# Keys and values of layer 1 in one 512-column product, the first output projection in two halves, a fourth weight slot

## The chip, the cores and the metric

The kernel runs on one core of one Trainium2 chip. A core has TensorE (PE, with its weight loads shown apart as PEld), VectorE (DVE), ScalarE (ACT), GpSimd (POOL), and SyncE (SP), whose queue issues most DMA transfers. Each engine takes its instructions in a fixed order. The metric is the device time of one execution in microseconds.

## The reference

Two transformer layers over 512 latent tokens and 256 context tokens, width 1024. Both normalize with adaptive scale and shift, project, attend, multiply by a SiLU gate, project out, normalize again and add to the stream. Layer 0 is differential attention with 8 heads, layer 1 grouped-query attention with 8 query heads and 2 key/value heads.

```
h  = rms_norm(x,  pre_g[i]) * (1.0 + scale)  + shift
hc = rms_norm(xc, pre_g[i]) * (1.0 + cscale) + cshift
# layer 0
q, k, v, z = split(h @ w_in)                 # heads with two maps each
o = softmax(q1 k1) v - lam * softmax(q2 k2) v
y = (rms_norm(o, subln_g) * (1 - lam_init) * silu(z)) @ w_out[0]
# layer 1
q, k, v, z = split(h @ w_in)                 # widths 1024, 256, 256, 1024
q, k = rms_norm(q, qk_g[0]), rms_norm(k, qk_g[1])
y = (softmax(rope(q) rope(k)) v * silu(z)) @ w_out[1]
# both
x  = x  + gate  * rms_norm(y,  post_g[i])
xc = xc + cgate * rms_norm(yc, post_g[i])    # layer 0 only
```

The output is the latent stream (512 x 1024) after layer 1.

## The kernel before

Every float32 product is made of three fast ones: an operand is split into a rounded part (`hi`) and the remainder (`lo`), and `mm3` issues hi·hi, hi·lo and lo·hi. `tmm` (L155) issues a single matmul, so most of PE's work has that line.

Weights come through `WStream`. A key stands for one block of 128 x 1024 values; `wsplit` loads it with SP into a raw tile (two buffers, tag `raw`), ACT casts it to `whi` (L225), and DVE subtracts to get `wlo` (L219). POOL does that for keys 9 and 11, in four pieces. A block needs a slot, a pair `whi`/`wlo`, from its load to `release`. Three slots exist throughout (`WBUFS`). A further one exists during the first projections (in the pool `st`), another from layer 0's output projection to the end of keys and values (pool `bp`, for those keys alone), and one more from there to the end of the kernel (pool `t1q`). Blocks are taken strictly in the order in which they were added.

Eight PSUM banks are used: four by themselves (`bk`; `pj` takes the one that was given back longest ago, `close` gives it back, `trp` takes one for a short time), and two pairs (`sc`, `sc2`) for scores and transposes.

Layer 0 runs as one flow over heads. `flow` walks lists of steps (scores S, transposes of probabilities T, products with values M, normalizing X, modulation vectors A) with costs, lags and due times from the constants at the top, and fills the time between due steps with pieces of projections (`fill0`: queries and keys `qk`, values `v`, gates `z`). The steps A compute adaptive vectors in twelve groups (`grp_mm`, L835); `gate0_finish` makes the gate of layer 0 from two of them per half: it loads `ada_b` and `post_g` into raw tiles, copies the row to all partitions with two matmuls per side (L1131, L1132), adds (L1133) and multiplies (L1134) on DVE for side 0 (latent) and 1 (context).

The code's order is not the engines' order: when the program is built, a scheduler places each engine's instructions by priority, and `tc.high_priority(offset=...)` moves a group ahead by that many. `HOT`, `HOT0`, `HOT1`, `WARM` and `PRI` are such offsets.

The output projection of layer 0 goes in column groups `OUTC`: 256, 256 and 512 columns, each for six token tiles of 128 rows. The first group is computed for the first seven of eight row blocks while the last head is still at work (`out_early`, into `o_pre`: two `sc` pairs for the latent tiles, two `bk` banks for the context tiles), and finished after it. Each group is multiplied by the gate on DVE and its squares are summed on ACT; `part_sum` on POOL adds the sums of the first two groups. After the third group a tile is normalized and added to the stream (`resid_a`, `resid_b`), and `h1_tr` transposes two tiles at a time (L1350) into the input of layer 1. The two context tiles (pair 2 of `h1_tr`, `t` in `KV`) are transposed among the key and value products.

The list `KV` orders that stage: `k` and `v` are 256-column products of one token tile (`proj_tok`, 8 row blocks x 3 matmuls), `t` transposes of context tiles, `c` transposes of finished keys (`k_tr`). Blocks 8 and 9 hold the key columns (4 row blocks of 256 columns each), 10 and 11 the value columns.

```
wk = (ws.get(8), ws.get(9))
...
o = pj(256)
run(proj_tok(o, wk if what == "k" else wv, m))
```

Then follow the queries of the first pair of heads and the attention flow of layer 1, built like that of layer 0, and its output projection (`OUTC1`).

Of the kernel before, what the change touches and what calls it, by code (L numbers as in the profile page):

```python
# [16 lines left out]
P = 128  # L17
# [11 lines left out]
HOT = -93  # L29
# [3 lines left out]
ACCN = (0, 0, 4, 2, 3, 2, 3, 4)  # L33
ACD = 0.54
FILL1 = (('q', 1), ('z', 0), ('z', 2), ('q', 2), ('z', 1), ('q', 3), ('z', 4), ('z', 5), ('z', 3), ('z', 6), ('z', 7))
HOT0 = (4682, 2421, 950, 3759)
HOT1 = (1476, 3151, 2600, 3663, 2938, 0)
WARM = 1817
AGB = 10
PRE = 16.26  # L40
# [3 lines left out]
KV = (('k', 0), ('k', 1), ('v', 0), ('k', 2), ('t', 0), ('k', 3), ('c', 0), ('v', 1), ('v', 2), ('t', 1), ('k', 4), ('c', 1), ('c', 2), ('k', 5), ('v', 3), ('v', 4), ('c', 3), ('c', 4), ('v', 5), ('c', 5))  # L44
SPL = 3.06
# [11 lines left out]
SLAG1 = 4.72  # L57
# [10 lines left out]
PRI = (1500, 218, 582, 400)  # L68
GFIN = (10, 13)
QLAG = 2.87  # L70
QTR = 5.35
# [6 lines left out]
RL = 3.57  # L78
# [9 lines left out]
def tile_backbone(  # L88
# [49 lines left out]
    def pj(n):  # L138
        i = lru.pop(0)
        o = banks[i][:, :n]  # L140
        held[id(o)] = (o, i)
        return o
# [136 lines left out]
    OUTC = ((0, 256), (256, 256), (512, 512))  # L279
# [9 lines left out]
    def wout_keys(layer, c, n):  # L289
        return [("o", layer, c, k) for k in range(KT * n // 1024)]  # L290

    def get_wout(layer, c, n):
        return [ws.get(k) for k in wout_keys(layer, c, n)]
# [518 lines left out]
    st_pool.close()  # L812

    gT = [None] * KT

    with tc.tile_pool(name="t0", bufs=1) as t0:
# [304 lines left out]
        def gate0_finish(half):  # L1121
            r = rows.pop((0, 4 + half))
            sl = slice(half * 512, half * 512 + 512)
            b = bcast(ada_b[0, 2 * D + half * 512:2 * D + half * 512 + 512])
            g = bcast(post_g[0, sl])
            rh, rl = (t0.tile([P, 512], F32R, tag="tmp", name=nm("rg"), bufs=3) for _ in range(2))
            nc.scalar.copy(rh, r)
            nc.vector.tensor_tensor(rl, r, f32(rh), ALU.subtract)
            for v in range(2):
                o = trp()  # L1130
                nc.tensor.matmul(o, selb[v], rh, start=True, stop=False)  # L1131
                nc.tensor.matmul(o, selb[v], rl, start=False, stop=True)  # L1132
                nc.vector.tensor_tensor(gate0[v][:, sl], o, b, ALU.add)  # L1133
                nc.vector.tensor_tensor(gate0[v][:, sl], gate0[v][:, sl], g, ALU.mult)  # L1134
# [135 lines left out]
    def proj_tok(o, w, t):  # L1270
        sl = slice(t * P, (t + 1) * P)
        for kt in range(KT):
            wh, wl = w[kt // 4]
            c = slice((kt % 4) * 256, (kt % 4) * 256 + 256)
            mm3(o, h1hi[:, kt, sl], h1lo[:, kt, sl], wh[:, c], wl[:, c], kt == 0, kt == KT - 1)
            yield 3 * 256 / 2400.0
# [8 lines left out]
    ws.extend(bp, WX[0], [*wout_keys(0, *OUTC[1]), *wout_keys(0, *OUTC[2]), 8, 9, 10, 11])  # L1285
# [7 lines left out]

    for qi, (c, n) in enumerate(OUTC[:2]):
        w = get_wout(0, c, n) if qi else w_o
        if qi == 0:
            for m in order:
                run(out_proj(o_pre[m], ghi, glo, w, m, n, KT - 1, KT))
        for m in order:
            v = 0 if m < NQ else 1  # L1300
            o = pj(n) if qi else o_pre[m]
            if qi:
                run(out_proj(o, ghi, glo, w, m, n))
            if qi == 0:
                u0[m] = hp.tile([P, 512], F32, tag="gT", name=nm("u0"), bufs=8)
                ss[m] = small(3)
            nc.vector.tensor_tensor(u0[m][:, c:c + n], o, gate0[v][:, c:c + n], ALU.mult)
            sumsq(ss[m][:, qi:qi + 1], o, n)
            if qi or m >= NQ:
                close(o)  # L1310
            if qi:
                part_sum(ss[m])
        ws.release(*wout_keys(0, c, n))
    c, n = OUTC[2]
# [63 lines left out]
    with tc.tile_pool(name="t1", bufs=1, side="right") as t1p:  # L1378
# [35 lines left out]
        wk = (ws.get(8), ws.get(9))  # L1414
# [24 lines left out]
        wv = None  # L1439
        for what, m in KV:  # L1440
            if what == "t":
                hot(h1_tr, 2, m)
            elif what == "c":
                k_tr(*ktr.pop(0))
            else:
                if what == "v" and wv is None:
                    wv = (ws.get(10), ws.get(11))
                o = pj(256)
                run(proj_tok(o, wk if what == "k" else wv, m))
                if late:  # L1450
                    k_rope(*late.pop())
                if what == "k":
                    late.append((m, o, head_rstd(o)))
                else:
                    nc.scalar.copy(vh[:, m, :], o)
                    nc.vector.tensor_tensor(vl[:, m, :], o, f32(vh[:, m, :]), ALU.subtract)
                    close(o)
# [3 lines left out]
        ws.extend(t1q, WX[1])  # L1461
# [354 lines left out]
```

## Time and profile before

| what | value |
| --- | --- |
| time, median of 3 runs (range) | 792.71 us (792.47 to 792.79) |
| time of the profiled execution | 792.77 us |
| its span, first to last instruction | 790.8 us |
| mean granted TensorE clock | 0.999 |
| DMA, mean over the span | 98 GB/s, 77.77 MB |
| PE's share of the chain that ended last | 89% |

The profile is of one execution. A page gives busy time of each engine, the costliest groups of instructions and the chain that ended last; further answers come from the same trace: busy time by stage, lists of waits, instructions in order of time. In a row of that last view stand start and length in us, engine, line, operation, tiles written and read, shape and count; in brackets the idle time before it and what ended it. Buffer numbers are left out in tile names. Ends of matmuls are modelled, starts are measured.

### The profile page before, as it was taken

The page shows a single profiled execution, that of the slowest core. Times are in us where ns is not written, and L with a number is a line of the kernel's source. Part 1 is how long each engine was busy: PE and PEld are TensorE (multiplying, and loading weights), DVE is VectorE, ACT ScalarE, POOL GpSimd, SP SyncE. Part 2 cuts the span into 40 slices and gives each one's busy share as a digit, 9 for nine tenths or more (in the row PEclk, how much of TensorE's full clock was granted, in tenths as well). Part 3 has the DMA queues.
Part 4 walks back from the last instruction along what each step waited for, and adds up shares of the span by engine and source line. Part 5 has one row for each costly group of instructions (what it writes and reads, how often), then busy time and mean ns, then how long its engine had stood idle before and what let it go on. Part 6 is the DMA issues. An engine that isn't in the chain of part 4 may idle for free.

```text
span 790.8 us, 14236 instructions
## 1 busy us (share of the span) xinstructions
PE 776.8 (98%) x5446; PEld 699.2 (88%) x5446; DVE 522.4 (66%) x940; ACT 455.4 (58%) x994; POOL 324.9 (41%) x434
## 2 busy tenths in 40 slices
PE   8999999999999999999999999999999999999996
PEld 6688888988887898888979998899999999989986
DVE  4666677786769637866578753567558977565634
ACT  5546546675575644775468843565456676676632
POOL 1121375663338542353425411585446654234101
PEclk9999999999999999999999999999999999999999
DMA  9934211131422322323330151041423512010102
GB/s 339 384 97 148 80 54 59 50 104 67 138 80 83 118 81 68 120 80 107 117 97 31 51 213 54 1 140 53 159 82 101 153 43 81 27 54 28 54 27 107
DMA packets 35092, 77.77 MB, mean 98 GB/s; under 512 B 3408, under 2 KB 10064, under 8 KB 35024
## 3 DMA queue, kind: packets, MB, share of 16 engines
q1 hardware_dynamic: 31168, 71.05, 26.9%
q10 hardware_dynamic: 3856, 5.81, 2.1%
q8 instruction: 43, 0.70, 0.3%
q14 instruction: 25, 0.20, 0.1%
HBM read 70.56 MB, written 2.10 MB: 92 GB/s over the span
## 4 chain that ended last, share of the span: by engine, by line
PE 89%; DVE 3%; ACT 3%; DMA 2%; POOL 1%; issue 1%; SPq 0%; DVEq 0%; ACTq 0%; POOLq 0%
PE bk L155 56%; PE sc L155 10%; PE bk L167 9%; PE sc L994 5%; PE bk L1059 3%; PE bk L1558 3%; PE bk L835 1%; DMA xnt<-in_xlT 1%; PE sc L1023 1%; POOL wlo L219 1%; DMA raw<-in_b_w 1%; DVE al L1063 1%; PE bk L406 1%; PE bk L407 1%; ACT p L1033 0%
## 5 line engine op out<-in xcount | busy, mean ns | idle before, releaser
L155 PE MATMUL bk<-whi,h 128*128 128x256 f32 (+1 forms) x1184 | 243.7, 299 | 0.0
L155 PE MATMUL bk<-h,whi 128*128 128x512 f32 (+2 forms) x864 | 227.9, 347 | 0.0
L155 PEld LDWEIGHTS bk<-whi,h 128*128 128x128 f32 x1184 | 191.8, 191 | 10.5 <-issue 4.0
L155 PE MATMUL bk<-wlo,h 128*128 128x256 f32 (+1 forms) x592 | 175.7, 299 | 0.0
L155 PEld LDWEIGHTS bk<-h,whi 128*128 128x128 f32 x864 | 149.9, 189 | 17.1 <-issue 2.9
L155 PE MATMUL bk<-h,wlo 128*128 128x512 f32 (+2 forms) x432 | 149.6, 346 | 0.0
L233 POOL TENSOR_SCALAR p<-p,sm 128x768 f32<-128x768 f32 (+1 forms) x80 | 71.7, 899 | 163.1 <-DVE sm L1005 63.9
L155 PEld LDWEIGHTS bk<-wlo,h 128*128 128x128 f32 x592 | 112.6, 191 | 3.8 <-issue 0.7
L219 DVE TENSOR_TENSOR wlo<-raw,whi 128x1024 fp32r<-128x1024 f32 (+1 forms) x66 | 80.7, 1226 | 34.4 <-ACT whi L225 34.3
L155 PEld LDWEIGHTS bk<-h,wlo 128*128 128x128 f32 x432 | 81.5, 189 | 7.1 <-issue 0.2
L225 ACT CAST whi<-raw 128x1024 fp32r<-128x1024 f32 x64 | 67.2, 1050 | 32.9 <-PE bk L155 27.8
L1002 ACT ACTIVATE p<-sc,sm 128x768 f32<-128x768 f32 (+1 forms) x68 | 59.5, 878 | 30.6 <-DVE sm L999 30.1
L999 DVE TENSOR_REDUCE sm<-sc 128x1 f32<-128x768 f32 (+1 forms) x68 | 60.3, 917 | 19.2 <-PE sc L994 19.2
L219 POOL TENSOR_TENSOR sz<-sz,za 128x192 f32<-128x192 f32 (+1 forms) x48 | 35.1, 752 | 65.8 <-ACT za L199 65.7
L1010 DVE SCALAR_TENSOR_TENSOR p<-p,sm,p 128x768 f32<-128x768 f32 (+1 forms) x34 | 40.3, 1186 | 7.4 <-POOL p L233 5.1
L994 PE MATMUL sc<-qk,qk 64*128 64x384 f32 (+1 forms) x396 | 43.8, 351 | 0.7 <-ACT p L1002 0.7
L1562 DVE TENSOR_TENSOR al<-bk,ah 128x512 fp32r<-128x512 f32 x48 | 32.1, 686 | 18.4 <-ACT ah L1561 18.2
L1062 ACT CAST ah<-bk 128x512 fp32r<-128x512 f32 x56 | 31.6, 589 | 19.0 <-PE bk L1059 16.6
L1063 DVE TENSOR_TENSOR al<-bk,ah 128x512 fp32r<-128x512 f32 x56 | 37.4, 683 | 6.7 <-ACT ah L1062 6.5
L1543 ACT ACTIVATE p<-sc,sm,qrs 128x768 f32<-128x768 f32 x32 | 31.9, 996 | 15.1 <-DVE sm L1540 8.9
L994 PEld LDWEIGHTS sc<-qk,qk 64*128 64x128 f32 x396 | 32.8, 184 | 7.7 <-issue 3.4
L1561 ACT CAST ah<-bk 128x512 fp32r<-128x512 f32 x48 | 26.9, 588 | 17.9 <-PE bk L1558 14.6
(240 smaller groups left out, 1492.6 us busy)
## 6 DMA issues: line engine op xcount, KB each, us to landing
raw<-in_a_w SPq DMA_DIRECT2D x28, 512.0 KB, 3.5
araw<-in_ada_w SPq DMA_DIRECT2D x12, 1024.0 KB, 5.2
raw<-in_b_w SPq DMA_DIRECT2D x20, 512.0 KB, 3.5
ag<-in_ada SPq DMA_DIRECT2D x16, 512.0 KB, 7.9
raw<-in_w_out SPq DMA_DIRECT2D x16, 512.0 KB, 3.5
sw<-qr ACTq DMA_DIRECT2D x32, 128.0 KB, 2.1
gw<-in_ada_w SPq DMA_DIRECT2D x8, 512.0 KB, 4.1
xnt<-in_xlT SPq DMA_DIRECT2D x4, 512.0 KB, 5.6
```

The source lines that it names most:

```text
L155: i = nc.tensor.matmul(o, a, b, start=start, stop=stop)
L167: nc.tensor.matmul(o, v[:, kt + e, c], a[:, e * 256:e * 256 + 256], start=first and i == 0, stop=last and i == 5)
L219: eng.tensor_tensor(dst[:, i:i + n], a[:, i:i + n], b[:, i:i + n], op)
L225: nc.scalar.copy(hi, r)
L233: (nc.vector if eng == "v" else nc.gpsimd).tensor_scalar(dst, src, s_, 1.0, ALU.mult, ALU.mult)
L994: prev = nc.tensor.matmul(sc[m][:, j if nk == T else m, :w], a[r, tok], b[r, c], start=i == 0, stop=i == 2)
L999: nc.vector.tensor_reduce(mx, scv, AX.XY if nk == T else AX.X, ALU.max, negate=True)
L1002: nc.scalar.activation(pv_, scv, AF.Exp, bias=mx, accum_out=l[:, m:m + 1])
L1010: nc.vector.scalar_tensor_tensor(ps_[0], pt, r, ps_[0], ALU.mult, ALU.add)
L1063: nc.vector.tensor_tensor(al, tr, f32(ah), ALU.subtract)
L1543: nc.scalar.activation(pt.rearrange("p (j n) -> p j n", j=2), scv, AF.Exp, scale=sr, bias=nmx, accum_out=l)
L1562: nc.vector.tensor_tensor(al, tr, f32(ah), ALU.subtract)
```

## The change

Four edits and new constants:

1. `OUTC` is (0, 512), (512, 512). The loop over the first two groups becomes one pass; `part_sum` there becomes one addition of epsilon. The first group now needs four weight blocks.
2. Blocks 8 to 11 hold keys and values side by side (2 row blocks of 512 columns each), one product gives both for a token tile, and `KV` has only `k`, `t` and `c`. `proj_tok` works out the columns per block from the number of blocks.
3. A fourth weight slot (`w4`) exists from the end of the first projections on; the one in `t1q` goes.
4. In `gate0_finish` the second matmul and the add get a priority offset of 3000.
5. Constants: priorities, due times and lags of both flows (below).

```diff
-HOT = -93
+HOT = 213
...
-ACCN = (0, 0, 4, 2, 3, 2, 3, 4)
-ACD = 0.54
+ACCN = (0, 0, 3, 2, 4, 1, 4, 4)
+ACD = 0.24
...
-HOT1 = (1476, 3151, 2600, 3663, 2938, 0)
+HOT1 = (1713, 4027, 2913, 3596, 2938, 0)
...
-PRE = 16.26
+PRE = 18.57
...
-KV = (('k', 0), ('k', 1), ('v', 0), ('k', 2), ('t', 0), ('k', 3), ('c', 0), ('v', 1), ('v', 2), ('t', 1), ('k', 4), ('c', 1), ('c', 2), ('k', 5), ('v', 3), ('v', 4), ('c', 3), ('c', 4), ('v', 5), ('c', 5))
-SPL = 3.06
+KV = (('k', 0), ('t', 0), ('k', 1), ('t', 1), ('k', 2), ('c', 0), ('k', 3), ('c', 1), ('k', 4), ('c', 2), ('k', 5), ('c', 3))
+SPL = 1.99
...
-SLAG1 = 4.72
+SLAG1 = 3.46
...
-PRI = (1500, 218, 582, 400)
+PRI = (1359, 218, 582, 400)
...
-QTR = 5.35
+QTR = 7.76
...
-RL = 3.57
+RL = 3.94
...
-    OUTC = ((0, 256), (256, 256), (512, 512))
+    OUTC = ((0, 512), (512, 512))
...
     st_pool.close()
+    ws.extend(ctx.enter_context(tc.tile_pool(name="w4", bufs=1)), 1)
...
                 nc.tensor.matmul(o, selb[v], rh, start=True, stop=False)
-                nc.tensor.matmul(o, selb[v], rl, start=False, stop=True)
-                nc.vector.tensor_tensor(gate0[v][:, sl], o, b, ALU.add)
+                with tc.high_priority(offset=3000):
+                    nc.tensor.matmul(o, selb[v], rl, start=False, stop=True)
+                    nc.vector.tensor_tensor(gate0[v][:, sl], o, b, ALU.add)
...
+        per = KT // len(w)
+        n = 1024 // per
         for kt in range(KT):
-            wh, wl = w[kt // 4]
-            c = slice((kt % 4) * 256, (kt % 4) * 256 + 256)
+            wh, wl = w[kt // per]
+            c = slice((kt % per) * n, (kt % per) * n + n)
...
-        wk = (ws.get(8), ws.get(9))
+        wkv = [ws.get(i) for i in (8, 9, 10, 11)]
...
-                if what == "v" and wv is None:
-                    wv = (ws.get(10), ws.get(11))
-                o = pj(256)
-                run(proj_tok(o, wk if what == "k" else wv, m))
+                o = pj(512)
+                run(proj_tok(o, wkv, m))
                 if late:
                     k_rope(*late.pop())
-                if what == "k":
-                    late.append((m, o, head_rstd(o)))
-                else:
-                    nc.scalar.copy(vh[:, m, :], o)
-                    nc.vector.tensor_tensor(vl[:, m, :], o, f32(vh[:, m, :]), ALU.subtract)
-                    close(o)
+                late.append((m, o, head_rstd(o)))
+                nc.scalar.copy(vh[:, m, :], o[:, 256:])
+                nc.vector.tensor_tensor(vl[:, m, :], o[:, 256:], f32(vh[:, m, :]), ALU.subtract)
+        k_rope(*late.pop())
+        while ktr:
+            k_tr(*ktr.pop(0))
...
-        ws.extend(t1q, WX[1])
```

How the order on the engines moves is shown at two places. The first is on DVE where the second half of layer 0's gate is made (`gate` 0 and 1 are the sides, `bk` the banks with the copied rows, `raw` the loaded vectors, `al` the remainders of transposed probabilities, `sc` scores). Before:

```order
L1034 RECIPROCAL sm_2691<-sm_2691 128x2
L1034 RECIPROCAL sm_2692<-sm_2692 128x2
L1036 TENSOR_TENSOR sm_2692<-sm_2692,nlam 128x2
L1133 TENSOR_TENSOR gate_0_691<-bk_70,raw_2736 128x512
L1133 TENSOR_TENSOR gate_1_692<-bk_71,raw_2736 128x512
L233 TENSOR_SCALAR gT_2416<-bk_69,subg 128x256
L1134 TENSOR_TENSOR gate_0_691<-gate_0_691,raw_2738 128x512
L1134 TENSOR_TENSOR gate_1_692<-gate_1_692,raw_2738 128x512
```

After:

```order
L1064 TENSOR_TENSOR al_2856<-bk_70,ah_2855 128x512
L1000 TENSOR_REDUCE sm_2939<-sc_72 128x1
L1135 TENSOR_TENSOR gate_0_700<-bk_68,raw_2910 128x512
L1000 TENSOR_REDUCE sm_2945<-sc_73 128x1
L1136 TENSOR_TENSOR gate_0_700<-gate_0_700,raw_2912 128x512
L1006 RECIPROCAL sm_2926<-sm_2926 128x1
L1064 TENSOR_TENSOR al_2884<-bk_70,ah_2883 128x512
L1006 RECIPROCAL sm_2926<-sm_2926 128x1
L1010 TENSOR_TENSOR sm_2926<-sm_2926,nlam 128x1
L1011 SCALAR_TENSOR_TENSOR p_2941<-p_2947,sm_2926,p_2941 128x768
L233 TENSOR_SCALAR gT_2423<-bk_69,subg 128x256
L1000 TENSOR_REDUCE sm_3042<-sc_72 128x1
```

The adds of the two sides, which stood next to each other behind the softmax sums, stand apart: side 0 between two row maxima (L1000), side 1 in the row that follows those shown.

The second place is on PE at the start of keys and values (`whi_5877`, `whi_5883` are blocks 8 and 9 before, `whi_5379`, `whi_5718`, `whi_5727` blocks 8 to 10 after, `h` the input of layer 1, `bk` the banks of the token tiles). Before:

```order
L1350 MATMUL sc_72<-ident,xn_5750 128x128 x4
L155 MATMUL bk_69<-whi_5877,h_687_5281 128x256
L155 MATMUL bk_71<-whi_5877,h_687_5281 128x256
L155 MATMUL bk_69<-wlo_5878,h_687_5281 128x256
L155 MATMUL bk_69<-whi_5877,h_688_5282 128x256
L155 MATMUL bk_69<-whi_5877,h_687_5281 128x256
L155 MATMUL bk_69<-wlo_5878,h_687_5281 128x256
```

After:

```order
L155 MATMUL bk_70<-whi_5718,h_690_5290 128x512
L155 MATMUL bk_70<-wlo_5719,h_690_5290 128x512
L155 MATMUL bk_70<-whi_5718,h_691_5291 128x512
L155 MATMUL bk_70<-whi_5718,h_690_5290 128x512
L155 MATMUL bk_68<-whi_5379,h_690_5290 128x512
L155 MATMUL bk_68<-wlo_5380,h_690_5290 128x512
L155 MATMUL bk_68<-whi_5379,h_691_5291 128x512
L155 MATMUL bk_68<-whi_5379,h_690_5290 128x512
L155 MATMUL bk_68<-wlo_5380,h_690_5290 128x512
L155 MATMUL bk_68<-whi_5379,h_691_5291 128x512
L155 MATMUL bk_70<-wlo_5719,h_690_5290 128x512
L155 MATMUL bk_70<-whi_5718,h_691_5291 128x512
```

Products of 256 columns that run through a tile's eight row blocks with two weight blocks have become products of 512 columns, and the first two token tiles take turns: while the remainder of block 9 (`wlo_5719`) is being split, the second tile (`bk_68`) runs on block 8.

More of the change, by code (lines that the diff above doesn't have):

```diff
@@ L1271, in proj_tok @@
         sl = slice(t * P, (t + 1) * P)
+        per = KT // len(w)
+        n = 1024 // per
         for kt in range(KT):
-            wh, wl = w[kt // 4]
-            c = slice((kt % 4) * 256, (kt % 4) * 256 + 256)
+            wh, wl = w[kt // per]
+            c = slice((kt % per) * n, (kt % per) * n + n)
             mm3(o, h1hi[:, kt, sl], h1lo[:, kt, sl], wh[:, c], wl[:, c], kt == 0, kt == KT - 1)
-            yield 3 * 256 / 2400.0
+            yield 3 * n / 2400.0
     x1 = [h1p.tile([P, D], F32, name=f"x1_{t}", bufs=1) for t in range(NQ)]
@@ L1284, in tile_backbone @@
     bp = bp_stack.enter_context(tc.tile_pool(name="bp", bufs=1))
-    ws.extend(bp, WX[0], [*wout_keys(0, *OUTC[1]), *wout_keys(0, *OUTC[2]), 8, 9, 10, 11])
+    ws.extend(bp, WX[0], [*wout_keys(0, *OUTC[-1]), 8, 9, 10, 11])
     for m in range(NQ):
@@ L1292, in sumsq @@
         nc.scalar.activation(jk, src, AF.Square, scale=D ** -0.5, accum_out=dst)
[L1294 to L1309, printed above, removed]
-                close(o)
[L1311 to L1314, printed above, removed]
+    c, n = OUTC[0]
+    w = w_o
+    for m in order:
+        run(out_proj(o_pre[m], ghi, glo, w, m, n, KT - 1, KT))
+    for m in order:
+        o = o_pre[m]
+        u0[m] = hp.tile([P, 512], F32, tag="gT", name=nm("u0"), bufs=8)
+        ss[m] = small(3)
+        nc.vector.tensor_tensor(u0[m], o, gate0[m // NQ][:, :n], ALU.mult)
+        sumsq(ss[m][:, 0:1], o, n)
+        if m >= NQ:
+            close(o)
+        nc.gpsimd.tensor_scalar(ss[m][:, 0:1], ss[m][:, 0:1], EPS, None, ALU.add)
+    ws.release(*wout_keys(0, c, n))
+    c, n = OUTC[1]
     w = get_wout(0, c, n)
@@ L1437, in k_rope @@
             ktr.append((m, kr))
-        wv = None
         for what, m in KV:
@@ L1778 @@
     for i in range(20):
-        if i < 12:
+        if i in (8, 9, 10, 11):
+            b_w[i] = bw[2 * i - 16:2 * i - 14, :, 8:12].transpose(1, 0, 2, 3).reshape(P, KT * P)
+        elif i < 8:
             pair, part = i // 2 * 2, i % 2
```

1 line of the change is left out of this document (removed).

## The prediction

> **What bounds the kernel now.** I read the page's first part, then busy time by stage, then the list of TensorE's waits, and last the order in time inside the stages that the change touches.
>
> ```profile
> PE 776.8 (98%) x5446; PEld 699.2 (88%) x5446; DVE 522.4 (66%) x940; ACT 455.4 (58%) x994; POOL 324.9 (41%) x434
> ```
>
> ```profile
> 0.00:40.00 40.00, 36.63 (x252) 27.14 (x253) 22.61 (x63) 20.86 (x42) 6.34 (x14) 1.00 0.97 358
> ...
> 80.00:160.00 80.00, 80.00 (x560) 69.68 (x558) 57.14 (x93) 46.29 (x100) 43.94 (x52) 1.00 0.18 60
> 160.00:240.00 80.00, 79.33 (x563) 68.80 (x560) 59.51 (x95) 48.17 (x100) 36.28 (x42) 1.00 0.30 98
> 240.00:320.00 80.00, 78.48 (x559) 69.44 (x558) 53.91 (x92) 43.56 (x94) 39.42 (x47) 1.00 0.26 84
> ...
> 500.00:530.00 30.00, 29.63 (x196) 26.75 (x194) 20.46 (x30) 20.89 (x53) 19.68 (x32) 1.00 0.28 92
> 530.00:560.00 30.00, 29.65 (x249) 29.65 (x250) 19.97 (x49) 14.72 (x43) 14.46 (x22) 1.00 0.22 70
> ...
> 760.00:791.00 31.00, 24.77 (x155) 22.28 (x153) 14.42 (x22) 9.00 (x25) 4.78 (x14) 0.96 0.24 86
> ```
>
> The first two figures after the stretch are its length and PE's busy time, the third from the end is the granted clock. PE is the bound in every stage: it idles 3.4 us at the start, 6.0 us at the end (the last row reaches 0.2 past the span), and of the 14.0 us in all (790.8 less 776.8) only 4.6 us between. The granted clock is 1.00, so nothing is lost there. A busy PE need not be a fast one, since ends of matmuls are modelled; the spacing of their starts tells more. In two stretches of the first output projection PE runs one form only:
>
> ```profile
> 469.71 0.28 PE L155 MATMUL bk<-wlo,h 128*128 128x256 f32 x1
> ...
> 479.80 0.28 PE L155 MATMUL bk<-wlo,h 128*128 128x256 f32 x1
> ```
>
> ```profile
> 481.69 0.39 PE L155 MATMUL bk<-wlo,h 128*128 128x512 f32 x1
> ...
> 494.61 0.39 PE L155 MATMUL bk<-wlo,h 128*128 128x512 f32 x1
> ```
>
> From the first row to the last, 84 matmuls of 256 columns start in 10.09 us, 120.1 ns each; 57 of 512 columns in 12.92 us, 226.7 ns each. So two of 256 cost 240.2 ns and one of 512 226.7: **13.5 ns a pair**. The few true waits are these:
>
> ```profile
> PE bk L1059 <- DVE gate L1133: 1.1, 1, 1.1
> ...
> PE sc L1350 <- POOL xn L1342: 0.7, 1, 0.7
> PE sc L994 <- ACT p L1002: 0.7, 1, 0.7
> PE bk L1059 <- DVE al L1063: 0.6, 1, 0.6
> PE bk L835 <- DVE al L1063: 0.6, 1, 0.6
> ```
>
> **The change, part by part.** The keys and values were 12 products of 24 matmuls with 256 columns and become 6 of 24 with 512. The two first quarters of the output projection, 2 x 6 x 24 with 256 columns, become 6 x 24 with 512. Together 576 matmuls become 288, with 288 weight loads fewer; no column is added or lost. At 13.5 ns a pair that is 288 x 13.5 = **3.9 us less** of PE, and as PE is dense on both sides of these stages it reaches the end. What could make it smaller is the spacing of 512 columns where waits lie between:
>
> ```profile
> 504.50 5.50 PE bk L155 x24
> ```
>
> This piece of the chain has 24 matmuls of 512 columns at 229 ns, so a pair saves 11 ns and the sum 3.2 us. These are my two ends; I take 3.9, because the stretch of 57 is the longer one.
>
> The Trainium skill, "TensorE: Matmul & The Clock Gate", section "Back-to-back issue gap", gives a warm spacing of N/2.4 + 2.5 ns: 109 ns for 256 columns, 216 ns for 512. By that a pair would save 2.6 ns and the whole 0.7 us, not 3.9. The trace disagrees at both sizes (120.1 and 226.7 ns), and the measurement decides.
>
> The evictions move with the products: DVE's multiply and ACT's sum of squares of the first half are 6 of 512 columns where 12 of 256 stood, and the POOL sum of two parts goes. DVE (66%) and ACT (58%) are no bound, and while they evict the six banks PE has the next half's first two tiles in the two other banks: 48 matmuls, 10.9 us at 226.7 ns. I cost this at nothing.
>
> **The start of keys and values** is a place to check, because one product now needs all four weight blocks (keys 8 to 11), where the first key product needed two. Before, the chain of waits runs there through the weights, and PE pays at its end:
>
> ```profile
> 499.99 0.44 PE sc L1350 x4
> ...
> 518.49 4.74 DMA raw<-in_b_w
> 523.24 0.02 issue
> 523.26 1.06 ACT whi L225
> ...
> 529.17 1.13 POOL xn L1342
> ```
>
> ```profile
> 515.34 3.13 POOL L219 TENSOR_TENSOR wlo<-raw,whi 128x256 fp32r<-128x256 f32 x4
> ...
> 524.39 2.83 POOL L219 TENSOR_TENSOR wlo<-raw,whi 128x256 fp32r<-128x256 f32 x4 [1.98 <-ACT whi L225]
> ```
>
> ```profile
> 517.00 0.48 PE L155 MATMUL bk<-whi,h 128*128 128x256 f32 x2
> ...
> 530.35 0.87 PE L1350 MATMUL sc<-ident,xn 128*128 128x128 f32 x6 [0.72 <-POOL xn L1342]
> ```
>
> The raw buffer of the last block (key 11) comes free when POOL has split key 9 (515.34 + 3.13); the block loads in 4.74 us, is cast in 1.06, POOL splits it in 2.83 and then norms the last context rows (xn), for which PE waits 0.72 us. With the fourth slot key 8 is loaded one release earlier, so PE starts on it at once. Key 9 may be cast after the last use of its slot, which by the order after lies 12 matmuls and 16 transposes (0.11 us each, by the four in 0.44) before the first product: 4.5 us, against 1.06 + 2.83 = 3.9 for its cast and split. The last block's load is then held only by the load of context rows ahead of it on SP's queue, which waits for the last transposes. If it starts 0.4 us into the first product, the block is there at 0.4 + 4.74 + 1.06 = 6.2 us. PE asks for it after 38 matmuls and 4 transposes, at 9.1 us: 2.9 us to spare. Before, the load began 1.5 us after the products (518.49 against 517.00), so xn comes 1.1 us earlier: 12.2 us after their start where it was 13.3. PE needs it 58 matmuls and 8 transposes, 14.0 us, after it. I take the 0.7 us wait as **gone**; its ends are 0 (kept) and -0.7.
>
> **The gate of layer 0.** The second matmul and the DVE add of each half now stand 3000 higher in priority, and the order shows gate 0 and gate 1 apart, with score work between. Before:
>
> ```profile
> 192.85 0.69 DVE L1133 TENSOR_TENSOR gate<-bk,raw 128x512 f32<-128x512 f32 x1 [1.52 <-DMA raw<-in_ada_b]
> 194.47 0.69 DVE L1134 TENSOR_TENSOR gate<-gate,raw 128x512 f32<-128x512 f32 x1 [0.94 <-DMA raw<-in_post_g]
> ```
>
> ```profile
> 242.86 1.28 DVE L1133 TENSOR_TENSOR gate<-bk,raw 128x512 f32<-128x512 f32 x2
> ```
>
> In the first half DVE stood 2.46 us for two loads, `al` came late and PE lost 0.6 us. In the second, two banks filled at 240 us were emptied only from 242.86 on, behind softmax work, and PE lost 1.1 us. With the add in front of that work a bank is free after its 0.69 us, and only one is held at a time. I take both as gone, **-1.7 us**. The ends are -1.7 and 0 (kept); no other wait of the list names the gate, and a loss is the last rival below.
>
> **The fourth slot and the constants** reorder the projections, the twelve ada steps (L835) and the attention of both layers: no operation is added, but each in-order queue gets a new sequence. The other waits of the list in the middle (0.7, 0.6, 0.6 and smaller, 2.2 of the 4.6 us) are taken as kept. New ones I can only bound by the density of the old: 4.6 us over the 720 us from 40 to 760 is 0.64 per 100 us, and the order differs most over some 300 us (about 190 to 370 and 580 to 690 us by what stands there), which gives 1.9. I take the middle between none and that, **+1.0**. One pair of ada steps stands closer than before, 47 rows of PE's order or some 7.8 us by the spacings above; the load between them takes 5.2 us, so it does not wait.
>
> ```profile
> araw<-in_ada_w SPq DMA_DIRECT2D x12, 1024.0 KB, 5.2
> ...
> raw<-in_ada_b SPq DMA_DIRECT2D x4, 256.0 KB, 3.8
> raw<-in_post_g SPq DMA_DIRECT2D x4, 256.0 KB, 3.9
> ```
>
> **The sum**, against the profiled execution: its 792.77 us are 790.8 of span and 2.0 around it, and it lies 0.06 above the median of 792.71. 792.77 - 3.9 - 0.7 - 1.7 + 1.0 = 787.5 us.
>
> **Rivals.**
> - The middle becomes denser still: all 4.6 us of idle time go. 792.77 - 3.9 - 4.6 = 784.3. For it: the waits are few and each has one cause. Against: 2.2 of the 4.6 us have causes (`al`, `p`) that no edit names.
> - The new sequence waits anew as much as the whole middle did: 792.77 - 3.9 - 2.4 + 4.6 = 791.1. For it: some 2,000 rows of PE's order stand elsewhere. Against: DVE and ACT have a third of their time free.
> - The first products starve. From POOL's start on key 9 to the normed rows it took 530.30 - 515.34 = 15.0 us before, and PE now needs them 14.0 us after the first product's start. If POOL starts on key 9 only with that product, PE waits 1.0, and one us more for each us later; 3 us late behind the norm of the latent rows (1.13) and ACT's evictions give 787.5 + 4.0 = 791.5. For it: POOL has no spare time in that chain. Against: the 0.6 us and the earlier load above.
> - A pair saves nothing, because the 13.5 ns belong to what lies between the matmuls in one stretch and not to their number: 792.77 - 2.4 + 1.0 = 791.4. Against: both stretches are neighbours with the same operands. By the spacing that the Trainium skill's page gives (0.7 us) this would read 790.7.
> - On the other side: the gate's add, now in front, makes the in-order DVE stand for both loads in both halves. They take 3.8 + 3.9 us, 15.4 in all; before, 2.46 us of standing cost PE 0.6, so 1.9 a half is covered and 15.4 - 3.7 = 11.7 reach PE: 787.5 + 11.7 = 799.2. It makes the kernel slower than before once DVE stands 5.3 + 3.7 = 9.0 us. For it: the priority. Against: the loads wait for raw buffers, which a fourth slot frees earlier.
>
> **How the numbers follow.** Forecast 787.5 (785.0 to 789.8) 0.68; denser 0.07; waits anew 0.09; starving 0.06; no saving 0.04; DVE standing 0.06. Faster by over 0.2% (under 791.1; 0.2% is about what a measurement of this kernel can tell from no change) are the first two, half of the waits anew (0.05) and half of the starving (0.03): 0.83. Within 0.2% are the other halves and the no-saving case: 0.11. Slower: 0.06, the standing DVE. The range goes up to 791.4 to take in the waits anew, the no-saving case and half of the starving, and down to 785.0: 0.84 in all, with the denser case and the standing DVE left out.
>
> **What would show it.** PE's count falls by 288 to 5158, loads too; 512-column rows in both stages start 227 ns apart; PE's busy time falls by about 3.9 us. The waits for gate L1135 and xn L1340 are missing from the list, or one of them is there and its step is wrong. New waits name the engine that came late. The forecast is wrong if 512 columns after the change start over 235 ns apart, or if PE idles over 7 us between 40 and 760 us.

## The result, and the profile after

The changed kernel takes 787.75 us (median of 6 runs, 787.70 to 787.86); the kernel before took 792.58 us beside it (792.32 to 792.79). The ratio is 0.9939, 95% interval 0.9927 to 0.9952: 4.8 us, or 0.6%, faster. The forecast was 787.5 us. The total came out as forecast, but not by the forecast's terms, as the runs below show.

The page's first part, span and busy time of each engine:

```profile
span 786.1 us, 13615 instructions
...
PE 771.3 (98%) x5158; PEld 683.3 (87%) x5158; DVE 526.6 (67%) x934; ACT 452.0 (58%) x982; POOL 321.8 (41%) x428
```

PE's count fell by 288 as predicted, its busy time by 5.5 us where 3.9 were forecast, and the span by 4.7. To see where, both traces are cut at the same places of the program: the first matmul of layer 0's output projection, the first one of keys and values, and the end of the second query product behind them. Busy time by stage, before and then after (length, then PE busy with its instructions):

```profile
40.00:444.52 404.52, 401.08 (x2832) 352.39 (x2831) 284.52 (x482) 240.92 (x502) 179.16 (x214) 1.00 0.27 88
444.52:517.00 72.48, 72.48 (x478) 66.36 (x478) 38.41 (x59) 37.49 (x92) 22.63 (x47) 1.00 0.24 83
517.00:561.36 44.36, 43.64 (x367) 43.44 (x366) 28.57 (x61) 23.95 (x68) 26.33 (x38) 1.00 0.36 119
561.36:790.80 229.44, 222.97 (x1526) 209.85 (x1524) 148.29 (x277) 132.20 (x293) 90.46 (x123) 1.00 0.22 72
```

```profile
40.00:442.14 402.14, 399.66 (x2833) 352.89 (x2832) 288.00 (x484) 240.89 (x503) 179.42 (x215) 1.00 0.27 90
442.14:512.91 70.77, 70.77 (x334) 58.81 (x334) 37.18 (x53) 35.54 (x80) 23.29 (x42) 1.00 0.23 83
512.91:556.61 43.70, 42.29 (x223) 35.71 (x222) 28.98 (x58) 22.51 (x67) 22.70 (x35) 1.00 0.31 104
556.61:786.10 229.49, 223.01 (x1526) 209.78 (x1524) 149.95 (x281) 132.26 (x293) 90.15 (x126) 0.99 0.23 73
```

Layer 0 up to its projection became 2.38 us shorter with the same matmuls; the projection 1.71 with 144 fewer; keys and values only 0.66, with 144 fewer; the rest is unchanged (+0.05). The list of TensorE's waits after, its longest:

```profile
PE bk L155 <- DVE sqx L618: 1.8, 3, 1.2
PE bk L155 <- DVE kl L1422: 1.4, 2, 0.9
PE bk L167 <- DVE al L1064: 1.2, 1, 1.2
...
PE sc L995 <- ACT p L1003: 0.7, 1, 0.7
PE bk L836 <- DVE al L1064: 0.6, 1, 0.6
```

The waits at the gate and for `xn` are gone. Two are new: 1.4 us for `kl`, the low part of the transposed keys, and 1.2 us for `al` at 96 us. (The waits for `sqx` stand in the list of before too, with 0.8 us. They lie in the first 40 us, in which both kernels get through the same work but for one matmul, so that the longer ones shorten nothing and cost next to nothing.) The `kl` wait in the order of time, PE first and DVE below:

```profile
536.91 0.60 PE L1418 MATMUL bk<-ident,kr 128*128 128x128 f32 x4
537.98 0.50 PE L155 MATMUL bk<-whi,h 128*128 128x512 f32 x1 [0.47 <-DVE kl L1422]
...
549.22 0.38 PE L1418 MATMUL bk<-ident,kn 128*128 128x128 f32 x2
550.54 0.39 PE L155 MATMUL bk<-whi,h 128*128 128x256 f32 x1 [0.94 <-DVE kl L1422]
```

```profile
547.61 2.54 DVE L219 TENSOR_TENSOR wlo<-raw,whi 128x1024 fp32r<-128x1024 f32 x2 [1.24 <-ACT whi L225]
550.07 0.42 DVE L1422 TENSOR_TENSOR kl<-bk,kh 128x256 fp32r<-128x256 f32 x1
```

A product does not read `kl`; it needs a bank. Two transposes of keys have just taken the last free ones, and they come back only when DVE has made `kl`, at the second place behind 2.54 us of weight splitting. Run e5 tests this reading.

### The profile page after: what moved, and what is told of

It is laid out like the page before. It is cut to its first block, busy times and chain, and to the rows that moved or that the text cites. A ratio compares the mean times of both kernels' runs of the same rounds, so it can differ in the third digit from the quotient of the medians.

```text
span 786.1 us, 13615 instructions
## 1 busy us (share of the span) xinstructions
PE 771.3 (98%) x5158; PEld 683.3 (87%) x5158; DVE 526.6 (67%) x934; ACT 452.0 (58%) x982; POOL 321.8 (41%) x428
## 4 chain that ended last, share of the span: by engine, by line
PE 93%; DVE 3%; ACT 3%; DMA 1%; issue 1%; POOL 0%; SPq 0%; DVEq 0%; ACTq 0%
PE bk L155 57%; PE sc L155 11%; PE bk L167 9%; PE sc L995 5%; PE bk L1060 3%; PE bk L1552 3%; PE bk L836 1%; PE sc L1024 1%; DMA xnt<-in_xlT 1%; ACT p L1003 1%; PE bk L406 1%; PE sc L1348 1%; PE bk L407 0%; PE bk L1488 0%; DVE wlo L219 0%
## 5 line engine op out<-in xcount | busy, mean ns | idle before, releaser
L155 PE MATMUL bk<-whi,h 128*128 128x256 f32 (+1 forms) x992 | 226.0, 317 | 1.4 <-DVE kl L1422 1.4
L155 PEld LDWEIGHTS bk<-whi,h 128*128 128x128 f32 x992 | 165.8, 190 | 17.4 <-issue 3.2
L155 PE MATMUL bk<-wlo,h 128*128 128x256 f32 (+1 forms) x496 | 155.5, 315 | 0.0
L155 PEld LDWEIGHTS bk<-wlo,h 128*128 128x128 f32 x496 | 94.0, 190 | 6.1 <-issue 0.7
L1000 DVE TENSOR_REDUCE sm<-sc 128x1 f32<-128x768 f32 (+1 forms) x68 | 60.3, 917 | 18.5 <-PE sc L995 18.3
```

The source lines that it names most:

```text
L155: i = nc.tensor.matmul(o, a, b, start=start, stop=stop)
L1000: nc.vector.tensor_reduce(mx, scv, AX.XY if nk == T else AX.X, ALU.max, negate=True)
```

## The experiments

All results in one table, ratios to the kernel before beside them; then each by its question.

| run | edit | us, median | ratio, 95% interval |
| --- | --- | --- | --- |
| after | the change | 787.75 | 0.9939, 0.9927 to 0.9952 |
| e1 | after, gate at normal priority | 787.89 | 0.9936, 0.9923 to 0.9950 |
| e2 | after, first half in quarters | 789.79 | 0.9960, 0.9947 to 0.9972 |
| e3 | after, keys and values in 256 columns | 792.15 | 0.9989, 0.9980 to 0.9998 |
| e4 | after, 288 matmuls split in place | 790.33 | 0.9967, 0.9954 to 0.9979 |
| e5 | after, key transposes in score banks | 785.75 | 0.9915, 0.9902 to 0.9929 |
| e6 | after, old constants | 793.38 | 1.0006, 0.9996 to 1.0015 |
| e7 | before, gate raised | 792.71 | 1.0002, 0.9994 to 1.0011 |
| e8 | before, fourth slot | 793.84 | 1.0017, 1.0008 to 1.0025 |
| e9 | as e3, transposes at old priority | 792.89 | 1.0001, 0.9992 to 1.0010 |
| e10 | before, keys and values in 512 columns | 794.93 | 1.0025, 1.0015 to 1.0035 |
| e11 | as e5, 288 matmuls split in place | 789.12 | 0.9954, 0.9942 to 0.9967 |
| e12 | before, new constants | 788.97 | 0.9953, 0.9939 to 0.9966 |

The kernel before ran beside them at 792.64 to 792.98 us.

### What is a pair worth: e2, e4, e11

```diff
-    OUTC = ((0, 512), (512, 512))
+    OUTC = ((0, 256), (256, 256), (512, 512))
```

(e2; the loop over the first two groups is that of before again.)

> The changed kernel with the first half of layer 0's output projection in two quarters again (144 pairs of 256 columns in place of 144 matmuls of 512), all else as changed. Theory (a pair costs 13.5 ns more than one of 512): 144 x 13.5 = 1.9 us more, 789.7 us; by the stage's own difference between the two traces, 1.7 us, 789.5. Rival (2.6 ns a pair, by the spacing that the Trainium skill, page TensorE: Matmul & The Clock Gate, section Back-to-back issue gap, states): 0.4 us more, 788.1.

Measured: 2.04 us more than after, 14.2 ns a pair. The stage in its trace:

```profile
442.16:514.66 72.50, 72.50 (x478) 66.31 (x478) 37.23 (x58) 37.12 (x91) 23.84 (x48) 1.00 0.22 81
```

That is 1.73 us longer than after's 70.77 (12.0 ns a pair) and the 72.48 of before again. PE is busy throughout in all three, so the evictions hide in either form.

```diff
+    def mm3s(o, ahi, alo, bhi, blo, start, stop):
+        for s in (slice(0, 256), slice(256, 512)):
+            mm3(o[:, s], ahi, alo, bhi[:, s], blo[:, s], start and s.start == 0, stop and s.start > 0)
```

(e4 and e11: `mm3s` in place of `mm3` for the first half of the projection and for keys and values.)

> The changed kernel with each of the 288 matmuls of 512 columns of the change split in place into two of 256: the same products, banks, evictions, slots and weights, only 288 matmuls and weight loads more. Theory (13.5 ns a pair belong to the number of matmuls): 3.9 us more, 791.6 us, and 120 ns from start to start where 227 stand now. Rival (the gain of these stages came from something else, such as fewer evictions or the order): less than 1 us more, under 788.7.

Measured: 2.58 us more, neither number. One of the two `kl` waits was missing from this run (0.9 us in place of 1.4), so the pairs cost more than that. From the projection to the second query product it took 117.29 us with PE idle for 0.94, after 114.47 with 1.41: without the idle time 3.3 us more. That asked for a kernel without the wait, e11:

> The kernel with the key transposes in the score banks (785.75 us) and each of the 288 matmuls of 512 columns split in place into two of 256. In that kernel no wait is left in the stage of keys and values, so that this prices the pairs alone. Theory (13.5 ns a pair, from the two longest pieces without waits): 3.9 us more, 789.6 us. Rival (with the interleaved transposes and changes of bank 512 columns start 229 to 230 ns apart, so 10 to 11 ns a pair): 2.9 to 3.2 us more, 788.8 us.

Measured against e5: 789.12 - 785.75 = 3.37 us, 11.7 ns a pair. From the projection to the second query product, with PE busy throughout in both, it took 115.87 us in place of 112.57: 3.30 us, 11.5 ns. (The two profiled spans, 787.2 and 784.2 us, differ by 3.0, since the part behind happens to be 0.2 longer in e5.) So the saving is real and belongs to the number of matmuls with their weight loads. It is some 11 to 12 ns a pair, nearer the prediction's low end (11 ns, 3.2 us) than the 13.5 it took. Undisturbed, 512 columns start as forecast; in after's keys and values 45 of them lie between these two rows, 227.1 ns each:

```profile
538.32 0.39 PE L155 MATMUL bk<-wlo,h 128*128 128x512 f32 x1
...
548.54 0.39 PE L155 MATMUL bk<-wlo,h 128*128 128x512 f32 x1
```

What is lost to the 13.5 ns probably lies at the changes between these stretches and transposes; no run takes it apart. The Trainium skill, "TensorE: Matmul & The Clock Gate", section "Back-to-back issue gap", gives N/2.4 + 2.5 ns, which it calls the gap of an isolated matmul; an estimate from it is 2.5 ns a pair and 0.7 us in all. e11 measured 3.37 and refutes that for these matmuls. The 131 ns that the section gives for 512 columns in a stream with weight loads aren't seen here either: the rows above show 227.1.

### The constants and the slot: e12, e8, e6

```diff
-HOT = -93
-ACCN = (0, 0, 4, 2, 3, 2, 3, 4)
-ACD = 0.54
+HOT = 213
+ACCN = (0, 0, 3, 2, 4, 1, 4, 4)
+ACD = 0.24
```

(e12: these and the other seven of the ten constants, in the kernel before; e6: the same ten turned back in the kernel after.)

> The kernel before with only the ten new constants (no slot, no merge, gate as before). Theory (the constants by themselves take the gate's two waits away and make the attention of layer 0 denser): the part up to the first output projection takes 442 to 443 us in place of 444.5, and no wait names the gate. Rival (the constants fit the slot's order only): 444.5 us or more there.

Measured: 788.97 us. The constants by themselves make 3.8 of the 4.8 us. Layer 0 in this run:

```profile
40.00:440.79 400.79, 399.52 (x2832) 352.03 (x2831) 287.00 (x482) 239.43 (x502) 179.38 (x214) 1.00 0.27 89
```

With the 2832 PE instructions of before the stage is 3.73 us shorter. 2.17 of it are idle time of PE that went (3.44 before, 1.27 now): the gate's two waits of 1.1 and 0.6 and one of 0.4 for `al` are no longer listed. The other 1.56 (401.08 to 399.52) stood inside "busy". Counted from the starts of the matmuls, 0.5 of it belongs to the same three waits: a row's shown end lies behind the time at which the next matmul would start (0.28 us long, but 0.12 apart for 256 columns), so each wait costs 0.16 us more than its listed idle time. Another 0.9 are pauses: starts that came 0.05 to 0.1 us later than is usual for their shape (109, 120, 173 and 227 ns for 128 to 512 columns), 161 where there were 173. Its wait for `xn` (0.7) stayed.

```diff
     st_pool.close()
+    ws.extend(ctx.enter_context(tc.tile_pool(name="w4", bufs=1)), 1)
...
-        ws.extend(t1q, WX[1])
```

> The kernel before with only the fourth weight slot, opened from layer 0 on (the slot that it opens for the queries of layer 1 goes in return). With the slot, the halves and the old constants the part up to the first output projection took 448.8 us (before: 444.5, after: 442.1). Theory (the slot brings blocks, and their casts and splits, earlier into the attention of layer 0, where the old constants don't provide for them): that part takes 447 us or more, the whole 795 us or more. Rival (the halves of the projection did it, whose first products hold whole banks): 444.5 us again. Of the wait for the normed context rows (`xn`, 0.7 us), which the prediction had the slot remove: it is gone if that step was right.

Measured: 793.84 us, 1.1 us more than before. The slot by itself costs time, though less than expected. In its profiled execution, the longest of eleven (795.75 us), the projection begins at 448.3 us, 3.8 later than before, of which about 1.5 are a drop of the granted clock told of in the last section. The new wait is for `al`, and it is 1.8 us here. DVE before and in e8 at that place:

```profile
93.22 0.95 DVE L999 TENSOR_REDUCE sm<-sc 128x1 f32<-128x768 f32 x1
94.08 0.68 DVE L1063 TENSOR_TENSOR al<-bk,ah 128x512 fp32r<-128x512 f32 x1
94.68 0.94 DVE L999 TENSOR_REDUCE sm<-sc 128x1 f32<-128x768 f32 x1
95.55 0.68 DVE L1063 TENSOR_TENSOR al<-bk,ah 128x512 fp32r<-128x512 f32 x1
```

```profile
93.52 1.21 DVE L219 TENSOR_TENSOR wlo<-raw,whi 128x1024 fp32r<-128x1024 f32 x1
94.66 1.81 DVE L1000 TENSOR_REDUCE sm<-sc 128x1 f32<-128x768 f32 x2
...
97.14 1.29 DVE L1064 TENSOR_TENSOR al<-bk,ah 128x512 fp32r<-128x512 f32 x2 [0.31 <-ACT ah L1063]
```

Before, `al` stood between two row reductions of the softmax; with the slot both reductions stand ahead of it, and it starts 3 us later. The wait for `xn` is gone from this run's list, and the stage of keys and values, with PE idle for 0.15 us instead of 0.72, is 0.6 us shorter:

```profile
520.79:564.54 43.75, 43.60 (x367) 43.40 (x366) 27.63 (x61) 23.97 (x67) 25.02 (x37) 1.00 0.37 122
```

In the old order of products, then, the slot takes this wait away. In the changed kernel it is not the slot that does it:

```profile
514.55 9.69 SPq L223 DMA_DIRECT2D raw<-in_b_w  x3
525.24 1.12 POOL L1340 TENSOR_SCALAR xn<-xn,sm 128x1024 f32<-128x1024 f32 x1
527.16 1.04 PE L1348 MATMUL sc<-ident,xn 128*128 128x128 f32 x8
```

The products begin there at 512.91. The last block's load starts 1.6 us behind that (forecast 0.4, before 1.5), and the normed rows are there after 13.5 us (forecast 12.2, before 13.3). But PE asks for them only after 14.2 us, as forecast (14.0), where before it asked after 12.6. The new order of products hides the wait; e10, which has that order without the slot, has no wait for `xn` either (PE asks there after 16.9 us).

> The changed kernel with the ten constants of the planner and of the priorities as before (the order of keys and values stays new, since the products need it). The part up to the first output projection took 2.4 us less after the change (444.5 to 442.1 us), and with the gate's priority undone it did so too. Theory (the new constants, with the slot, made that gain): 2.4 us more, 790.1 us, with waits for `al` and the gate in layer 0. Rival G (with the old constants the gate's priority is what removes its two waits of 1.7 us): under 788.7 us, and no wait names the gate's add. Rival S (the fourth slot alone does it): within 0.4 us of 787.75.

Measured: 793.38 us, its shortest execution 791.64: 5.6 and 3.9 us more than after. Both the gate's waits and a doubled wait for `al` are back, although the gate stands at its new priority:

```profile
PE bk L167 <- DVE al L1064: 2.2, 2, 1.8
...
PE bk L1060 <- DVE gate L1135: 1.1, 1, 1.1
...
PE bk L1060 <- DVE al L1064: 0.6, 1, 0.6
```

Rivals G and S fall. The theory holds in its direction, but the loss is larger than its 2.4 us; about 1.5 us of it in the profiled execution are again a drop of the clock (at 99 us).

### The gate's priority: e1, e7

```diff
-                with tc.high_priority(offset=3000):
-                    nc.tensor.matmul(o, selb[v], rl, start=False, stop=True)
-                    nc.vector.tensor_tensor(gate0[v][:, sl], o, b, ALU.add)
+                nc.tensor.matmul(o, selb[v], rl, start=False, stop=True)
+                nc.vector.tensor_tensor(gate0[v][:, sl], o, b, ALU.add)
```

(e1; e7 is the reverse of it in the kernel before.)

> The changed kernel with one part undone: the second matmul and the add of each gate half stand at normal priority again. Theory (the prediction's third term): DVE stands or comes late at the gate again, so waits of TensorE that end at the gate's add or at `al` around it come back, up to 1.7 us: 788.5 to 789.5 us. Rival (the old waits belonged to the old order, which the new constants and the fourth slot have replaced anyway): 787.75 us to 0.4, and no wait names the gate's add.

> The kernel before with only the gate's second matmul and add raised in priority. Theory (the prediction's third term): the two waits at the gate, 1.1 and 0.6 us, go: 791.0 us. Rival 1 (it does nothing): 792.6 us. Rival 2 (the raised add makes DVE stand for the loads in front of the softmax): more than 792.7 us, with longer waits of TensorE for `al`.

Measured: e1 787.89 us, 0.14 more than after, and no wait names the gate; e7 792.71 us, against 792.64 beside it. In e7 both waits stay (1.0 and 0.8 us), and the add stands where it stood, behind the same softmax work:

```profile
242.75 0.23 DVE L1036 TENSOR_TENSOR sm<-sm,nlam 128x2 f32<-128x2 f32 x1
242.90 1.27 DVE L1134 TENSOR_TENSOR gate<-bk,raw 128x512 f32<-128x512 f32 x2
```

It began at 242.86 before. The raised priority does nothing that can be measured in either surrounding; the rival of e1 and rival 1 of e7 hold. In after the first add of each half stands at

```profile
205.54 0.68 DVE L1135 TENSOR_TENSOR gate<-bk,raw 128x512 f32<-128x512 f32 x1
253.06 0.68 DVE L1135 TENSOR_TENSOR gate<-bk,raw 128x512 f32<-128x512 f32 x1
```

That is 10 to 13 us later than before, with no standing for a load, and the second add of each half follows 6.6 and 8.1 us behind. In e1 and e12 the four adds stand at the same places to within 1.5 us. So the constants moved them.

### Keys and values: e3, e9, e10

> The changed kernel with keys and values as 12 products of 256 columns in their old order again, weights packed as before, all else as changed. Theory A (the merge saved its 1.9 us and the 0.7 us wait for the normed rows, as predicted): 2.6 us more, 790.4 us. Theory B (from the trace after: the merge brought two waits of 1.4 us together for the banks of the key transposes, so only 0.65 us of it reached the end): 788.4 us, with TensorE's waits for `kl` gone and the wait for `xn` back.

> The changed kernel with keys and values as 12 products of 256 columns in their old order, as in the run of that name, and with the priority of the transposes between them as before (-93 in place of 213), all else as changed. That run lost 4.4 us, of which 2.4 us were new waits for `h` and `kn` that the kernel before doesn't have. Theory (the waits came from the new priority in the old order): they go, and what is left is the merge's own worth: 0.65 us by the two traces, 788.4 us, or 2.6 us by the prediction, 790.4 us. Rival (the waits belong to 256 columns with the new slot): 792 us again.

```diff
-                o = pj(512)
-                run(proj_tok(o, wkv, m))
+                o = pj(256)
+                run(proj_tok(o, wk if what == "k" else wv, m))
```

(With the old `KV` and the old packing; e9 also with `HOT = -93`.) Measured: e3 792.15 us, e9 792.89 us, 4.4 and 5.1 us more than after. That is beyond both theories of e3; e9's theory falls and its rival holds. (Four of e3's eleven executions, with a mean clock of 0.996, have the drop told of in the last section; the others took 791.17 to 792.18 us.) The waits only changed names. E3's longest, 1.6 us, is for `h`, rows that the product reads; e9's in this stage are:

```profile
PE bk L155 <- DVE kn L1428: 1.1, 1, 1.1
PE bk L155 <- DVE vl L1454: 0.9, 1, 0.9
PE bk L155 <- DVE kl L1422: 0.8, 1, 0.8
```

These three are waits for a product bank, since the product reads none of the three tiles. Undoing the merge inside the new surroundings therefore doesn't price the merge; probably the old order of products fits the old surroundings only. The other side, the merge alone:

> The kernel before with only keys and values in one product of 512 columns (weights packed for it, the new order of products, transposes and key transposes). The prediction's terms by themselves: 144 pairs at 13.5 ns and the 0.7 us wait, 2.6 us less than before, 790.1 us. Theory from the trace after (the merge pays 1.4 us for banks behind the key transposes, and a pair saves some 11 ns): 1.6 + 0.7 - 1.4 = 0.9 us less, 791.8 us, with waits for `kl` of about 1.4 us. Without the fourth slot the wait for the first blocks or for `xn` may stay: then 792.5 us.

Measured: 794.93 us, 2.2 us slower than before, where the prediction's terms gave 790.1, the theory from the trace after 791.8 and its case without the slot 792.5: all three miss. Its executions range from 793.42 to 795.5; the shorter ones have a mean granted clock of 0.999, the longer ones 0.995 to 0.997. The stage:

```profile
516.90:563.55 46.65, 43.90 (x224) 37.27 (x223) 30.33 (x61) 23.58 (x68) 25.75 (x38) 0.96 0.37 123
```

PE idles for 2.75 us, again for banks, 1.9 of them behind `kl`. About 1.5 us of the stage are the drop of the clock that follows (0.96 in this row). So in the kernel before the merge lost: even the shortest executions are 0.7 us slower.

### The bank wait taken away: e5

```diff
-            tr = trp()
+            tr = sc2()[:, 0, :]
```

(In `k_tr`: the key transposes go to a score bank, free there.)

> The changed kernel with the transposes of the keys written into the score banks (free at that point of the program) in place of the four product banks. Theory (the two waits for `kl`, 1.4 us, are waits for a product bank: each product of keys and values holds its bank until its keys are normed, and two transposes take the last free ones): both go, 787.75 - 1.4 = 786.3 us. Rival (DVE and ACT are late there anyway, behind the split of the weights for the queries): another wait takes their place, 787.2 to 787.8 us.

Measured: 785.75 us (785.71 to 786.11), 2.0 us less than after and 6.9 less than the 792.64 beside it: faster than both kernels. No wait is left in the stage:

```profile
512.71:554.51 41.80, 41.80 (x223) 35.60 (x222) 27.94 (x56) 20.91 (x62) 22.32 (x34) 1.00 0.31 104
```

PE is busy for all of 41.80 us, 1.9 less than after (1.41 of idle time and 0.49 of pauses inside "busy"). Against the 44.36 of before that is 2.56 us: nearly the 2.6 us (1.9 for the pairs, 0.7 for `xn`) that the prediction gave this stage. The theory holds, with more than its 1.4 us, and the rival falls.

## Why the prediction was right, and where it was not

- **The pairs, -3.9 us.** Right in mechanism, somewhat large. In the projection 1.71 us arrived (1.94 forecast); e11 prices all 288 at 3.3 to 3.4. The term was sized by the longest undisturbed stretches; its low end of 3.2 was nearer.
- **Evictions at nothing.** Right for the projection, where PE idles in no form. For keys and values the step was missing: I followed the weight blocks and the normed rows there and not the banks. A product of 512 columns keeps its bank until keys are normed and values are split, and the transposes of keys take the others. That wait of 1.4 us (2.0 us by e5) left 0.66 of the 2.6 us.
- **The wait for `xn`, -0.7 us.** The wait went, but not as told. The step "If it starts 0.4 us into the first product" failed: the last block's load started 1.6 us in, and the rows came as late as before (13.5 us, before 13.3). What held was the other half of the comparison, that PE asks for them only after 14 us; 1.8 us to spare were forecast and 0.8 were there. The slot removes the wait in the old order (e8 against e12), and isn't needed for it in the new one (e10).
- **The gate, -1.7 us.** The waits went, but the step that the raised priority puts the add in front of the softmax work failed: e7 raises it and they stay, e1 lowers it and they don't return. It was the constants that removed them (e12 against e6): with them the adds come 10 to 13 us later and apart. Which of the ten does it stays open.
- **Slot and constants, +1.0 us.** The largest error, and of the wrong sign for the constants. Alone they bring -3.8 us (e12), the slot alone +1.1 (e8), with a new `al` wait. The density of old waits bounded what a new order could lose; what it could gain was put at the "denser" rival with 0.07, and bounded by the visible 4.6 us of idle time. E12 took 1.56 us out of time shown as busy, which that bound left out. In the changed kernel PE's idle time from 40 to 760 us hardly fell, from 4.6 to 4.3 us: most of the gain, that of the pairs included, came out of "busy".
- **Rivals.** The slower one (DVE standing at the add) did not occur: the raised priority doesn't move the add, and where the constants put it DVE stands for no load. The starving one neither: the list has no wait for weights there. "A pair saves nothing" is refuted by e11. Of the new waits that another feared, 2.2 us came (1.4 for `kl`, 0.8 more for `al`).
- **What was to show it.** The count of 5158, and PE's idle time between 40 and 760 us below the 7 us that would have shown it wrong (4.3), and the 227 ns of 512 columns hold. PE's busy time fell by 5.5 and not 3.9. Of this, 1.1 us lie in the first 40 us (36.63 to 35.56) and were only exchanged for the longer `sqx` waits; the 1.4 us in layer 0 are the real sign that something beside the pairs had been gained.

The total of 787.5 was thus right by luck, by errors that cancel: by stage the forecast was too poor by some 1.7 us in layer 0 (2.38 against 1.7 less the 1.0 of new waits, if all of these are put there) and too good by 1.9 in keys and values (0.66 against 2.6). What the single edits bring does not add up: constants -3.8, slot +1.1, gate 0.1, keys and values +2.2 (each alone on the kernel before), and the halves -2.0 (by undoing them) make -2.4, the change -4.8. (With e10's executions without the clock drop, +0.7 for keys and values, they make -3.9.) Taken the other way, with the new constants in place the other edits together bring only 1.2 us more (e12's 788.97 to 787.75), where the prediction had 4.6 for pairs and `xn`. The rest is interplay: the merge loses alone (e10), yet undoing it costs 4.4 and 5.1 (e3, e9). Which of the ten constants matter, and why the merge fits the new surroundings better, was not tried.

## What to carry to other kernels

Fewer and wider matmuls are worth their spacing, here 11 to 12 ns for each that goes, but a wider product also holds its PSUM bank for longer: follow the banks, with all that takes one, as closely as the weights. When a change comes with newly fitted constants, run those alone on the old kernel first: here they were most of the gain, and the raised priority that looked like the cause of two vanished waits did nothing. Idle time of the bound engine is not the limit of what a better order can gain, since short pauses between its instructions count as busy. And a wait that goes as forecast may have gone for another reason: look at when the thing came and when it was asked for.

## What the runs showed of the hardware

A wait of 1.8 us cost about 1.5 us more behind it. In e8, PE stood for 1.79 us for `al`; each microsecond from there on (the third figure from the end is the granted clock):

```profile
97.00:98.00 1.00, 0.12 (x1) 0.12 (x2) 0.86 (x2) 1.00 (x4) 0.83 (x1) 1.00 0.47 188
98.00:99.00 1.00, 1.00 (x7) 1.00 (x8) 1.00 (x3) 1.00 (x4) 0.00 (x0) 0.73 0.00 0
99.00:100.00 1.00, 1.00 (x7) 1.00 (x6) 0.86 (x5) 0.25 (x1) 0.00 (x0) 0.50 0.00 0
100.00:101.00 1.00, 1.00 (x6) 1.00 (x6) 1.00 (x1) 0.00 (x0) 0.00 (x0) 0.50 0.00 0
101.00:102.00 1.00, 1.00 (x5) 0.81 (x4) 0.01 (x1) 0.00 (x0) 0.00 (x0) 0.56 0.00 0
102.00:103.00 1.00, 1.00 (x6) 0.82 (x5) 0.00 (x0) 0.00 (x0) 0.00 (x0) 1.00 0.00 0
```

```profile
98.46 0.62 PE L167 MATMUL bk<-al,vhi 128*128 128x256 f32 x2
...
101.87 0.40 PE L155 MATMUL bk<-h,wlo 128*128 128x512 f32 x1
```

From 98.46 to 101.87, 3.41 us, matmuls start 213 ns apart for 256 columns and 430 for 512, where before shows 120 and 235 for the same work (96.16 to 98.55). Over the 14 of them that loses 1.5 us. The same 3.4 us at 0.50 follow waits in e3, e6 and e10. The waits of 1.2 us in after are followed by no such drop. Not every execution has one: e8's range from 793.70 to 795.75 us, the longest with a mean clock of 0.996.

The clock records of the kept traces say more. In all 14, the clock changes only at whole steps of 3.413 us after its first rise (in e8 after 27, at 98.46, and 28). Counted in these steps, the clock fell behind each in which PE idled 1.9 us or more, the end of the kernel included, and behind none with up to 1.6; of the four steps with 1.8 it fell behind three. So what counts here is the idle time within one step, with the limit near half of it, and a wait that is split between two steps may cost nothing more. That would explain why only some executions have a drop; no run was made for it. The Trainium skill, "TensorE: Matmul & The Clock Gate", section "Part 1: The HAM clock gate (the "warmup" mystery)", has half clock as the lower of the two states of its table, and windows of 3.4 us; the rows agree with both. It puts the fall to half clock behind at least one idle window of about 3.4 us; here 1.8 us of idle time in one were enough.
